# FoX attention: values multiplied as float16 halves, and the sums of the probabilities taken on TensorE in quarters of its columns

## The chip, the cores and the metric

One core of a Trainium2 chip runs the whole program in one launch. The metric is device time in microseconds (us), the median over runs. The engines are called by the profile's names: PE is TensorE (PEld its weight loads), DVE is VectorE, ACT is ScalarE, POOL is GpSimd, SP issues the DMAs. Each takes its own instructions in order and waits on semaphores for the others.

## What is computed

A decoder layer with three mixers side by side. The change concerns one of them, the forgetting attention (FoX): 8 heads of 64, 2048 queries (and 16 meta tokens ahead of them), swept in blocks.

```python
s = jnp.einsum('bhqd,bhkd->bhqk', qi, kf) * scale + cqi[..., None] - c[:, :, None, :]
mask = (kpos[None, :] <= qpos[:, None]) & valid[None, :]
p = jax.nn.softmax(jnp.where(mask, s, NEG), axis=-1)
return jnp.einsum('bhqk,bhkd->bhqd', p, vf)      # times silu(fg) afterwards
```

So every block needs the probabilities p, their product with the values v, and their row sums.

## The kernel before

The program runs in stages: norms and projections, the GLA mixer, the RG-LRU mixer, then FoX, then the output projection. `hybrid_kernel` writes a list of jobs; `merge` interleaves the main part of a job (for FoX, `fox_attend`) with the preparation of the next (`fox_prepare`) and, through the FoX stage, with a slow side job that prepares the output weights (`wout_ready`). A scheduler then sets each engine's order. The FoX stage has 16 jobs: 4 head pairs p, and for each 4 chunks c of 512 queries.

`fox_attend(p, c)` runs over blocks j of 128 keys, 4c+5 of them, so 5, 9, 13 and 17, and 176 in all. The last five of a chunk see fewer queries: 400, 272, 144 and 16 columns in place of 512. For each j:

- PE makes the logits of both heads in the PSUM pair `sq` (L1280, float16 high and low halves of keys and queries, and the forget terms `KX`), and adds the mask (L1286) on the diagonal. `sq` has one buffer, so the next j's logits wait for the exp of this one.
- ACT takes the exp of both heads into `pt`, float32, 1024 wide, a ring of three (L1288).
- DVE, and POOL for head 1 of every even j, add `pt` into the running sums `za` (L1293, L1296).
- PE multiplies values and probabilities, float32, into the PSUM bank `fv`: one matmul a head (L1304), each using 64 of the array's 128 columns. It does so for block j-2, behind the logits of block j; the last three come together at the end of the chunk.

After the last j, ACT copies the product (L1310), POOL multiplies it by the gate (L1311), PE sums `za` over its partitions (L1315, float32, the PSUM bank `fx`), and ACT copies that row (L506). Through a small DRAM buffer it is spread over the partitions, inverted on DVE (L1317, L1318), sent back and broadcast to `rz`, which POOL multiplies in (L1323).

`fox_prepare` for the next chunk makes the keys, queries and values (L485, L497), the values leaving PSUM by one ACT operation with a scale (L1173). It also finds each query's row maximum: PE makes logits in the pair `mq` (L1220, L1224, one buffer), DVE adds the forget terms and takes the maximum (L1228). The maxima are transposed through the bank `fx` (L1240) and sent by six small DMAs (L1251) into `QA`, where the attend's last logit matmuls read them.

## Time and profile before

| | us |
|---|---|
| median of 3 runs | 2014.05 (2011.25 to 2014.08) |
| the profiled execution | 2012.92 |
| its span | 2011.2 |
| the FoX stage in it, first logits to last sums | 915.2 to 1713.6, so 798.4 |

About 1.7 us lie outside the span. The profile's busy times and idle times are of this one execution. A matmul's end is modelled, so groups of matmuls of one kind show some 0.1 us more than the time to the next start; what a group takes from the engine is read from start to start. In the views below a pair of heads that runs at the same time shows as two matmuls, and a float32 matmul leaves two records, one for each of its two passes.

### The profile page before, as it was taken

The page shows a single profiled execution, that of the slowest core. Times are in us where ns is not written, and L with a number is a line of the kernel's source. Part 1 is how long each engine was busy: PE and PEld are TensorE (multiplying, and loading weights), DVE is VectorE, ACT ScalarE, POOL GpSimd, SP SyncE. Part 2 cuts the span into 40 slices and gives each one's busy share as a digit, 9 for nine tenths or more (in the row PEclk, how much of TensorE's full clock was granted, in tenths as well). Part 3 has the DMA queues.
Part 4 walks back from the last instruction along what each step waited for, and adds up shares of the span by engine and source line. Part 5 has one row for each costly group of instructions (what it writes and reads, how often), then busy time and mean ns, then how long its engine had stood idle before and what let it go on. Part 6 is the DMA issues. An engine that isn't in the chain of part 4 may idle for free.

```text
span 2011.2 us, 39461 instructions
## 1 busy us (share of the span) xinstructions
PE 1896.8 (94%) x15988; PEld 987.0 (49%) x15988; DVE 1271.7 (63%) x2834; ACT 1010.8 (50%) x1561; POOL 583.0 (29%) x564
## 2 busy tenths in 40 slices
PE   6889999999999999989999998899999988999998
PEld 5456666665555555545434442354335422444443
DVE  6756363444688778674565367756874665567664
ACT  7745553344888888762345233533442335444441
POOL 3434232332433333330122112221121124443432
PEclk9889999999999999999999999999999998999999
DMA  6200120211211110121132104321332108733411
GB/s 226 71 7 29 41 86 28 75 44 34 74 43 45 43 43 22 43 72 44 59 95 70 34 28 115 116 70 64 90 97 69 43 22 304 221 114 115 130 49 63
DMA packets 116134, 152.69 MB, mean 76 GB/s; under 512 B 18792, under 2 KB 75816, under 8 KB 115952
## 3 DMA queue, kind: packets, MB, share of 16 engines
q1 hardware_dynamic: 115952, 150.18, 23.4%
q8 instruction: 125, 2.05, 0.4%
q14 instruction: 57, 0.47, 0.1%
HBM read 108.71 MB, written 41.33 MB: 75 GB/s over the span
## 4 chain that ended last, share of the span: by engine, by line
PE 70%; DVE 9%; ACT 6%; issue 3%; POOL 3%; DMA 3%; SPq 0%; ACTq 0%; POOLq 0%; DVEq 0%
PE pj L485 28%; PE pj L1572 14%; PE pj L497 6%; PE fv L1304 6%; PE sq L1280 5%; PE mq L1220 2%; PE st L590 2%; DVE mj L1228 2%; ACT pt L1288 1%; PE gs L1028 1%; PE pv L1062 1%; DVE za L1296 1%; PE fx L1315 1%; DVE xc L563 1%; PE mq L1224 1%
## 5 line engine op out<-in xcount | busy, mean ns | idle before, releaser
L485 PE MATMUL pj<-xhl,whl 128*128 128x512 f16 (+3 forms) x3960 | 812.1, 356 | 10.8 <-ACT whl L437 6.3
L485 PEld LDWEIGHTS <-whl 128*128 128x128 f16 x3984 | 364.0, 98 | 396.0 <-issue 73.6
L1288 ACT ACTIVATE pt<-sq,consts 128x1024 f32<-128x1024 f32 (+4 forms) x176 | 163.3, 928 | 268.6 <-PE sq L1286 90.6
L1296 POOL TENSOR_TENSOR za<-za,pt 128x512 f32<-128x512 f32 (+1 forms) x80 | 101.0, 1262 | 548.1 <-ACT pt L1288 499.4
L1228 DVE CUSTOM_DVE_ANT_0 mj<-mq,CB 128x512 bf16<-128x512 f32 (+4 forms) x344 | 192.7, 580 | 63.0 <-PE mq L1220 31.1
L1572 PEld LDWEIGHTS <-whl 128*128 128x128 f16 x1344 | 130.6, 98 | 160.8 <-issue 4.5
L497 PEld LDWEIGHTS <-xhl 128*128 128x128 f16 (+1 forms) x3264 | 192.8, 100 | 33.6 <-issue 29.3
L497 PE MATMUL pj<-whl,xhl 128*128 128x128 f16 (+1 forms) x3024 | 197.6, 224 | 0.0
L1296 DVE TENSOR_TENSOR za<-za,pt 128x512 f32<-128x512 f32 (+3 forms) x208 | 121.5, 607 | 93.3 <-ACT pt L1288 90.2
L1304 PE MATMUL fv<-pt,fv 128*64 128x512 f32 (+4 forms) x688 | 175.1, 545 | 0.0
L1572 PE MATMUL pj<-xhl,whl 128*128 128x512 f16 x768 | 168.7, 380 | 0.0
L1280 PE MATMUL sq<-QA,KA 64*128 64x512 f16 (+4 forms) x1032 | 128.2, 344 | 12.3 <-ACT pt L1288 12.2
L1572 PE MATMUL pj<-ts,whl 128*128 128x512 f16 x576 | 125.7, 379 | 0.0
L563 DVE SCALAR_TENSOR_TENSOR xc<-lx,consts,xc 128x448 f32<-128x448 f32 (+1 forms) x120 | 93.7, 781 | 3.6
L1556 POOL TENSOR_TENSOR o<-o,xt 128x512 f32<-128x512 f32 x31 | 51.6, 1683 | 120.4 <-issue 91.7
L1538 ACT ACTIVATE sqo<-o 128x512 bf16<-128x512 f32 x32 | 20.1, 630 | 128.3 <-DVE o L1532 128.3
L1280 PEld LDWEIGHTS <-KA 64*128 64x128 f16 (+1 forms) x1032 | 40.3, 94 | 87.3 <-issue 65.5
L521 ACT ACTIVATE gate<-pj,consts 128x512 f32<-128x512 f32 (+2 forms) x72 | 46.1, 640 | 70.6 <-PE pj L485 58.5
L1578 DVE SCALAR_TENSOR_TENSOR o<-pj,consts,o 128x512 f32<-128x512 f32 x56 | 41.0, 744 | 60.5 <-PE pj L1572 56.3
L1220 PE MATMUL mq<-KA,QA 64*128 64x512 f16 (+4 forms) x344 | 60.8, 343 | 17.5 <-DVE consts L1228 15.1
L598 POOL TENSOR_TENSOR v<-a 128x448 f32<-128x448 f32 (+1 forms) x40 | 38.9, 973 | 129.4 <-ACT a L596 129.3
L522 DVE SCALAR_TENSOR_TENSOR gate<-gate,pj 128x512 f32<-128x512 f32 (+2 forms) x72 | 45.2, 627 | 40.8 <-ACT gate L521 40.7
(260 smaller groups left out, 2802.8 us busy)
## 6 DMA issues: line engine op xcount, KB each, us to landing
wr<-in_w_out_dram SPq DMA_DIRECT2D x64, 256.0 KB
y<-yD SPq DMA_DIRECT2D x32, 512.0 KB
raw<-in_w_grp_dram SPq DMA_DIRECT2D x28, 512.0 KB
wD<-ws SPq DMA_DIRECT2D x56, 256.0 KB
CB<-c32D SPq DMA_DIRECT2D x32, 256.0 KB
rawf<-in_w_grp_dram SPq DMA_DIRECT2D x16, 512.0 KB
xhl<-wD SPq DMA_DIRECT2D x16, 512.0 KB
xt<-in_x_dram SPq DMA_DIRECT2D x16, 512.0 KB
```

Of the source, the lines that this page charges most:

```text
L485: nc.tensor.matmul(out=ps, lhsT=a[:, kt, 0:m], rhs=b[:, kt, u0:u0 + n], start=i == 0, stop=i == 23)
L497: nc.tensor.matmul(out=ps, lhsT=a[:, kt, u0:u0 + m], rhs=b[:, kt, :], start=i == 0, stop=i == 23)
L521: k.act = nc.scalar.activation(out, ps, AF.Tanh, scale=hinv).ins
L563: nc.vector.scalar_tensor_tensor(out=xc, in0=lx[:, j:j + n], scalar=cw(j), in1=xc, op0=ALU.mult, op1=ALU.add)
L1220: nc.tensor.matmul(out=ps[h][:, 0:n], lhsT=qh[hs, P * i:P * i + P], rhs=d.hi[pc][hs, 0:n], start=True, stop=pc < c)
L1228: nc.vector.tensor_tensor_reduce(out=junk[:, h, 0:n], in0=ps[h][:, 0:n], in1=d.cb[pc][:, h, 0:n], scale=1.0, scalar=-3e38, op0=ALU.add, op ...
L1280: nc.tensor.matmul(out=sp[0:m, h, off:], lhsT=a[j // 4][hs, kk], rhs=b[hs, off:], start=i == 0, stop=i == 3 and d < 0)
L1288: k.exp = nc.scalar.activation(pt[0:m, :, off:], sp[0:m, :, off:], AF.Exp, scale=K.esc[0:m]).ins
L1296: eng.tensor_tensor(out=za[h][0:m, off:], in0=za[h][0:m, off:], in1=pt[0:m, h, off:], op=ALU.add)
L1304: nc.tensor.matmul(out=pv[hs, off1:], lhsT=V1[0:m1, j1 % 4, hs], rhs=pt1[0:m1, h, off1:], start=j1 == 0, stop=j1 == nj - 1)
L1556: eng.tensor_tensor(out=o, in0=o, in1=xt[:, h, :], op=ALU.add)
L1572: nc.tensor.matmul(out=ps, lhsT=a[:, kt, :], rhs=w[b + kt // 4][:, :, kt % 4, :], start=kt + j == 0, stop=(kt, j) == (KT - 1, 2))
```

## The change

The probabilities are lifted by 2^14 in the exp (a bias of 14 ln 2) and split on the spot: ACT copies them to float16 (`ph`, high half) and DVE subtracts to get the low half. The values are split in the same way when they leave PSUM, scaled by 2^-15. PE multiplies three of the four products of halves, and a float16 matrix of ones takes the sums: four matmuls a block (two halves by two heads), each using 32 of the array's columns and writing a quarter of a new PSUM bank `zb`. The adds on DVE and POOL, the buffers `za` and the sum matmuls at the chunk's end go; the bank `fx` becomes `zb`, and the transposed maxima go through `mq`. The end of a chunk sends four rows instead of two and adds two halves on DVE. The ring of `pt` shrinks to two, `ph` has three. In the output stage the loads of the last three weight blocks are ordered behind the send of these rows.

```diff
-PBUFS = {"pj": 2, "mx": 2, "st": 2, "pv": 2, "fx": 1, "fv": 1}
+PBUFS = {"pj": 2, "mx": 2, "st": 2, "pv": 2, "zb": 1, "fv": 1}
...
-    nc.scalar.activation(V[0:m, :, :], ps[0:m, 0:nb, :], AF.Copy, scale=wv[2][0:m])
+    split_pair(k, ps[0:m, 0:nb, :], V[0:m, 0], V[0:m, 1])
...
-    ps = bank(k, "fx")
+    ps = pair(k, "mq")[:, 0, :]
     nc.tensor.transpose(out=ps[0:8, 0:P], in_=mm, identity=k.ident)
...
-    za = [unit(k, "ZA", [P, CH], name="za") for _ in range(2)]
+    zb = bank(k, "zb")
...
-        pt = k.wk.tile([P, 2, CH], F32, name="pt", tag="PT", bufs=3)
+        pt = k.wk.tile([P, 2, CH], F32, name="pt", tag="PT", bufs=2)
+        ph = k.wk.tile([P, 2, 2, CH], F16, name="ph", tag="PH", bufs=3)
...
-        k.exp = nc.scalar.activation(pt[0:m, :, off:], sp[0:m, :, off:], AF.Exp, scale=K.esc[0:m]).ins
-        for h in range(2):
-            if j == 1:
...
-            elif j > 1:
-                eng = nc.gpsimd if h == 1 and j % 2 == 0 else nc.vector
-                eng.tensor_tensor(out=za[h][0:m, off:], in0=za[h][0:m, off:], in1=pt[0:m, h, off:], op=ALU.add)
...
+        nc.scalar.activation(pt[0:m, :, off:], sp[0:m, :, off:], AF.Exp, scale=K.esc[0:m], bias=k.lift[0:m])
+        k.exp = nc.scalar.copy(out=ph[0:m, 0, :, off:], in_=pt[0:m, :, off:]).ins
+        nc.vector.tensor_tensor(ph[0:m, 1, :, off:], pt[0:m, :, off:], ph[0:m, 0, :, off:], op=ALU.subtract)
+        todo.append((j, m, off, ph, V))
...
-                    nc.tensor.matmul(out=pv[hs, off1:], lhsT=V1[0:m1, j1 % 4, hs], rhs=pt1[0:m1, h, off1:],
-                                     start=j1 == 0, stop=j1 == nj - 1)
+                for i, (zv, zp) in enumerate(((0, 0), (1, 0), (0, 1))):
+                    for h in range(2):
+                        hs = slice(64 * h, 64 * h + 64)
+                        nc.tensor.matmul(out=pv[hs, off1:], lhsT=V1[0:m1, zv, j1 % 4, hs], rhs=ph1[0:m1, zp, h, off1:],
+                                         start=j1 == 0 and i == 0, stop=j1 == nj - 1 and i == 2)
+
+                for z in range(2):
+                    for h in range(2):
+                        r = slice(64 * z + 32 * h, 64 * z + 32 * h + 32)
+                        nc.tensor.matmul(out=zb[r, off1:], lhsT=k.onesh[0:m1], rhs=ph1[0:m1, z, h, off1:],
+                                         start=j1 == 0, stop=j1 == nj - 1)
...
-        nc.tensor.matmul(out=zp[hs, :], lhsT=k.ones[:, 0:64], rhs=za[h], start=True, stop=True)
-    D, zt = rows_spread(k, NCH * p + c, zp)
...
+    nc.scalar.copy(out=zs, in_=zb)
+    for z in range(2):
+        for h in range(2):
+            r = 64 * z + 32 * h
+            k.zdma = nc.sync.dma_start(out=D[z, h:h + 1, :], in_=zs[r:r + 1, :]).ins
...
+    nc.vector.tensor_tensor(zt[0], zt[0], zt[1], op=ALU.add)
...
-    k.mark = k.load
+    k.mark = k.zdma
```

The scheduler's new order is shown at three places. The first is PE in the middle of a late chunk, at a block with 400 columns. Before, in this place, the two float32 matmuls of the values (`fv`) follow the mask matmuls of a later block (L1286) and the next projection (L485) follows them:

```order
L1280 LDWEIGHTS KX
L1280 MATMUL sq<-QA,KX 128x144
L1286 LDWEIGHTS consts
L1286 MATMUL sq<-consts 128x128
L1304 MATMUL fv<-pt,fv 64x400 x2
L485 LDWEIGHTS whl
L485 MATMUL pj<-xhl,whl 128x512
```

Now the six float16 matmuls (of which the last two stand here) are followed by four of 32 columns into `zb`, and then by the next row-maximum logits (L1227, which was L1220):

```order
L1305 LDWEIGHTS fv
L1305 MATMUL fv<-ph,fv 64x400
L1311 LDWEIGHTS consts
L1311 MATMUL zb<-ph,consts 32x400
L1227 LDWEIGHTS QA
L1227 MATMUL mq<-KA,QA 128x512
```

Rows that repeat are left out: the pairs L1305 stand six times there and the pairs L1311 four times, each matmul with a weight load of its own. Where PE went from the values to other work at once, it now passes through a third form of matmul.

The second place is ACT in the last chunk of the stage, where the exps (`pt`) stand between the halves of the output stage's first operands (`whl`). Before:

```order
L1288 ACTIVATE pt<-sq,consts 128x1024
L1443 ACTIVATE whl<-y,consts 128x1024
L1288 ACTIVATE pt<-sq,consts 128x2x400
L1443 ACTIVATE whl<-y,consts 128x1024
L1443 ACTIVATE whl<-s_19338,consts 128x1024
L1288 ACTIVATE pt<-sq,consts 128x2x272
```

After, a cast to `ph` behind each exp (L1296 is the exp, L1460 the halves):

```order
L1296 ACTIVATE pt<-sq,consts 128x1024
L1297 CAST ph<-pt 128x1024
L1460 ACTIVATE whl<-y,consts 128x1024
L1296 ACTIVATE pt<-sq,consts 128x2x400
L1297 CAST ph<-pt 128x2x400
L1460 ACTIVATE whl<-y,consts 128x1024
```

The exp of 400 columns now has a cast and a half ahead of it instead of a half alone.

The third place is DVE in a late chunk, where the sums stand among the row maxima (`mj`) and the halves of the output weights (`ws`). Before:

```order
L1444 SCALAR_TENSOR_TENSOR ws<-wr,consts,ws 128x512
L1228 ISA mj,consts<-mq,CB 128x512
L1228 ISA consts 128x1
L1317 RECIPROCAL consts<-consts 128x8
L1318 TENSOR_SCALAR consts<-consts 128x8
L1293 TENSOR_TENSOR za<-pt 128x512 x2
```

After, one subtraction for both heads (L1298, here at a block of 144 columns) in the place of two adds, and the low half of the values (L1106) as a new operation; L1235 was L1228, L1461 was L1444:

```order
L1106 SCALAR_TENSOR_TENSOR fv<-pj,fv 128x512
L1298 TENSOR_TENSOR ph<-pt,ph 128x2x144
L1235 ISA mj,consts<-mq,CB 128x512
L1235 ISA consts 128x1
L1461 SCALAR_TENSOR_TENSOR ws<-wr,consts,ws 128x512
```

A row maximum that PE waits for can now stand behind a subtraction that itself waits for a cast.

## Rows read from the trace of the kernel before

**Rows 1.** Page of the profile, head and part 1: busy time, share of the span.

```profile
span 2011.2 us, 39461 instructions
PE 1896.8 (94%) x15988; PEld 987.0 (49%) x15988; DVE 1271.7 (63%) x2834; ACT 1010.8 (50%) x1561; POOL 583.0 (29%) x564
```

**Rows 2.** Stretches: length, then busy PE, PEld, DVE, ACT, POOL, granted clock, DMA.

```profile
1143.10:1189.60 46.50, 46.39 (x338) 19.91 (x338) 24.11 (x77) 15.04 (x26) 7.30 (x6) 1.00 0.04 13
1189.60:1245.10 55.50, 50.06 (x321) 17.29 (x322) 41.51 (x122) 23.41 (x32) 10.53 (x9) 0.94 0.30 92
...
1648.30:1713.60 65.30, 49.85 (x263) 14.56 (x262) 35.73 (x60) 31.02 (x37) 24.91 (x15) 0.85 0.74 250
915.20:1713.60 798.40, 755.09 (x5487) 314.08 (x5486) 498.70 (x1352) 311.78 (x454) 156.01 (x123) 0.98 0.27 84
```

**Rows 3.** Waits of PE in the FoX stage: us in total, times, longest.

```profile
PE mq L1220 <- DVE consts L1228: 13.9, 14, 3.7
PE sq L1280 <- ACT pt L1288: 12.2, 14, 3.0
```

**Rows 4.** Timeline of PE, one block: start, us, line, form, count.

```profile
1297.89 0.38 PE L1280 MATMUL sq<-QA,KX 64*128 64x512 bf16 x2
1298.20 1.08 PE L1304 MATMUL fv<-pt,fv 128*64 128x512 f32 x4
1299.21 0.96 PE L497 MATMUL pj<-whl,xhl 128*128 128x128 f16 x14
```

**Rows 5.** Timeline of PE, one head of a block by itself.

```profile
1290.87 1.07 PE L1304 MATMUL fv<-pt,fv 128*64 128x512 f32 x2
```

**Rows 6.** FoX stage, L1304, L1315 (PE, PEld), L1296 (DVE, POOL) alone, in turn.

```profile
915.20:1713.60 798.40, 176.01 (x704) 39.99 (x704) 0.98 0.27 84
...
915.20:1713.60 798.40, 19.24 (x64) 3.56 (x64) 0.98 0.27 84
...
915.20:1713.60 798.40, 121.48 (x208) 100.98 (x80) 0.98 0.27 84
```

**Rows 7.** Timeline of PE in earlier stages: matmuls of 48 and of 32 columns.

```profile
83.24 2.81 PE L633 MATMUL pj<-xhl,whl 128*48 128x256 f16 x48
85.98 0.82 PE L485 MATMUL pj<-xhl,whl 128*128 128x512 f16 x3
...
135.67 0.87 PE L1028 MATMUL gs<-lv 64*32 64x32 f32 x64 [0.33 <-DVE ac L1031]
```

**Rows 8.** Groups by line and form: count, busy us, mean ns, idle before.

```profile
L542 ACT CAST wrih<-wri 128x1024 fp32r<-128x1024 f32 x2 | 2.1, 1040 | 8.3 <-DMA wri<-in_w_i_dram 8.3
...
L1488 DVE TENSOR_TENSOR s<-s,y 128x1024 f32<-128x1024 f32 x8 | 9.7, 1216 | 6.8 <-POOL s L1487 6.7
...
L1100 DVE SCALAR_TENSOR_TENSOR KA<-pj,KA 128x512 f16<-128x512 f32 x16 | 11.0, 690 | 41.4 <-ACT KA L1099 41.4
```

**Rows 9.** Timeline of a late chunk: DVE alone, and beside POOL.

```profile
1308.15 0.74 DVE L1444 SCALAR_TENSOR_TENSOR ws<-wt,consts,ws 128x512 f16<-128x512 f32 x1
...
1310.26 1.78 POOL L1296 TENSOR_TENSOR za<-za,pt 128x512 f32<-128x512 f32 x1 [5.51 <-ACT pt L1288]
1310.83 1.76 DVE L1444 SCALAR_TENSOR_TENSOR ws<-wr,consts,ws 128x512 f16<-128x512 f32 x1
```

**Rows 10.** Timeline of the last chunk; in brackets the idle time before, and its cause.

```profile
1668.17 0.82 PE L1280 MATMUL sq<-QA,KA 64*128 64x512 f16 x6 [0.26 <-ACT pt L1288]
...
1669.30 1.11 ACT L1288 ACTIVATE pt<-sq,consts 128x1024 f32<-128x1024 f32 x1 [1.18 <-PE sq L1280]
...
1679.59 1.27 POOL L1323 TENSOR_TENSOR fo<-fo,rz 128x512 f32<-128x512 f32 x1 [4.72 <-DMA rz<-rowD]
...
1682.12 1.11 ACT L1288 ACTIVATE pt<-sq,consts 128x1024 f32<-128x1024 f32 x1 [3.15 <-POOL za L1296]
...
1683.28 0.82 PE L1280 MATMUL sq<-QA,KA 64*128 64x512 f16 x6 [2.21 <-ACT pt L1288]
```

**Rows 11.** Timeline of SP's queue as the output stage begins.

```profile
1723.65 0.91 SPq L1412 DMA_DIRECT2D ts<-wD  x2
```

More of the change, by code (lines that the diff above doesn't have):

```diff
@@ L261, in setup_constants @@
     nc.vector.memset(k.onesb, 1.0)
+    k.onesh = carve(k, 16).bitcast(F16)
+    nc.vector.memset(k.onesh, 1.0)
+    k.lift = carve(k, 1)
+    nc.vector.memset(k.lift, 14.0 * math.log(2.0))
     k.eps = carve(k, 1)
@@ L508, in rows_spread @@
         nc.sync.dma_start(out=D[0, h:h + 1, :], in_=zs[64 * h:64 * h + 1, :])
-    zt = small(k, "zt", [P, 8], bufs=2)
+    zt = small(k, "zt", [P, 8], bufs=4)
     nc.sync.dma_start(out=zt, in_=D[0].rearrange("h (q e) -> (h q) e", e=8))
@@ L1109, in fox_begin @@
     last = unit(k, "M", [P, 7 * NM + P], name="last")
-    d.lastV = last[:, 7 * NM:].rearrange("p (b v) -> p b v", b=1)
+    d.lastV = last[:, 7 * NM:].bitcast(F16).rearrange("p (z b v) -> p z b v", z=2, v=P)
     d.last = [last[:, NM // 2 * i:NM // 2 * (i + 1)].bitcast(F16) for i in range(2)]
```

27 lines of the change are left out of this document (13 added, 14 removed).

## The prediction, made before the changed kernel was run

> **What bounds the kernel now.** I read the shares of the page first: PE is busy 94% of the span, no other engine over 63% [rows 1]. The change touches the FoX stage alone, 798.4 us, so I cut that stage at the copies that end the chunks (L1310). Chunks of 5 and 9 blocks are PE's alone: the one from 1143.1 is 46.50 us long with PE busy 46.39, DVE 24.11 and ACT 15.04. Chunks of 13 blocks are less clear: 55.50 us with PE 50.06 and DVE 41.51. The last chunk, which has no next attention chunk to prepare, is bound by latency: 65.30 us to the end of the stage, PE 49.85, granted clock 0.85 [rows 2]. Over the stage PE is busy 755.09, DVE 498.70, ACT 311.78, POOL 156.01. Then the waits: PE waits most for DVE's row maxima (13.9 us) and for the exp (12.2 us) [rows 3]. So two questions decide: does the change take time from PE's own stream, and do the new operations on ACT and DVE make PE wait more.
>
> **PE's stream.** Logits, values and projection follow each other there without a wait [rows 4]: the float32 values of both heads take 1298.20 to 1299.21, 1.01 us, while the logit pair ahead, 512 columns of float16, takes 0.31 to the next start. Six such matmuls in three pairs take 0.66 up to it, 0.22 a pair, so 0.09 of the 0.31 is a change of the array's shape (64 rows to 64 columns). I find 0.09 to 0.10 at each change of that kind. The float32 pair itself is then 0.91, two passes of 0.43 and one weight load. One head by itself is as long as two together: 1.07 with its tail for one head, 1.08 for two [rows 4, 5]. So halves of the columns run at the same time when they stand next to each other, and a pair that the scheduler has torn apart costs a second 0.91.
>
> After, a full block has three float16 pairs at 0.216 and one quartet. That float16 halves run together is in the trace too: 48 matmuls of 48 columns by 256 take 83.24 to 85.98, 2.74 us [rows 7]. Less one change that is 0.110 a pair, the time of 256 columns once, with their weight loads hidden. For quarters there is only one poor row: 64 float32 passes of 32 columns by 32 in 0.87, which one quarter at a time, with both row halves at once, would need some 0.85 for without tail and change (32 times 0.027, from 0.43 for 512). I take the quartet as 0.216, since with the tail the row leaves about 0.7; the bounds are below.
>
> Sums, in blocks of 512: 112 blocks are full and 16 each have 400, 272, 144 and 16 columns; in pairs of float16 that is 30.1 us for all 176. Unbroken, before: the values 127 and the sums at the chunk ends (L1315) 16 times 0.91, 141 us. Unbroken, after: 30.1 times four, 120 us. To this come the torn groups, which I counted in the two orders: 18 us before, 12 after. So 159 becomes 132, **27 us less**. (The busy times, 176.01 and 19.24 [rows 6], are larger since they hold the tails.) Against it stand the changes of shape: a quartet is a third form beside halves of rows and halves of columns, and in the orders PE changes shape 845 times in the stage before and 1126 times after: 281 times 0.096 are **27 us more**. Logit pairs torn apart more often add 4. PE's own stream comes out at **+4 us**, where the work of the matmuls alone would promise a loss of 27.
>
> On the changes of shape the Trainium skill ("TensorEngine Tiling (Array Packing)", Key Properties) says that a change of the tiling mode, not of the tile alone, drains the engine; by that rule each quartet pays for coming and going. The row agrees, with 0.09 us for a change. Were only the changes between halves and quarters of columns free, 274 of them, the stream would come out at 22 us less; nothing in the rows suggests so.
>
> By chunks this +4 is uneven, and that matters, as PE's time counts fully only where PE binds. Counted in the same way, a chunk of 5 blocks gains 1 us of stream, one of 9 loses 2, one of 13 gains 3 to 5 (its quartets are torn most), one of 17 loses 3 to 4. Those of 13 have 5 us of room in the row above, so part of their gain is free.
>
> **ACT.** New: 176 casts. The nearest row is the cast of 1024 columns from SBUF, 1040 ns [rows 8]: 112 full ones are 116 us, the narrower ones some 34, together 150. ACT goes from 312 to 462 of 798 us, not the bound. Its cover is plainest in the last chunk, where ACT does nothing but exps for ten blocks: 1.11 us of exp, then 1.18 idle until the next logits [rows 10]. A cast of 1.04 fits, with 0.14 to spare; without that idle time it would cost 1.04 a block. The other copies there (squares and halves for the output stage) have no such room, and I put 2 us on the last chunk. The exp's bias operand has no row; it lies between nothing and 0.1 us an exp, and the idle 1.18 covers both ends but for the last 0.04.
>
> **DVE and POOL.** Out: 121.48 us of adds on DVE and 100.98 on POOL [rows 6]. In, on DVE: subtractions of 1024 columns at 1216 ns [rows 8], 112 times 1.22 is 137, the narrower ones 35; the low halves of the values, 16 at 690 ns and 4 small ones, 12; the adds and multiplies at chunk ends, about 7. DVE would go from 499 to 568. But POOL's adds slowed DVE: the same operation is 0.74 us alone and 1.76 beside an add on POOL [rows 9]. With all 80 adds gone that is between nothing and 80 times 1.02, 82 us; most of DVE's operations read PSUM and keep their time, and I take 25 off. So 543, 68%, spread as before. ACT also no longer waits for POOL: in the last chunk POOL stands 4.72 us for a DMA, the add behind it holds the `pt` buffer, the exp waits 3.15 and PE 2.21 [rows 10]. That wait goes; next late there is the chain of the sums' row on DVE, which stalls the same queue once a chunk while its DMA lands, as before. Of the 12.2 us that PE waits for exps in the stage [rows 3] I count two such places out of sixteen chunks' ends, **-4 us**.
>
> **What is added as waits.** The subtraction of block j waits for the cast, which waits for the exp; behind it in DVE's queue stand the row maxima, for which PE waits in `mq` [rows 3]. The exp of j+2 waits for the subtraction of j, with a ring of two where the adds had three. PE's value matmuls of j come two blocks later and need the low half. With 13.9 and 12.2 us of such waits now, and a chain longer by 1.04, I add a quarter to a third, **+7 us**; the bounds are nothing and the rival below. The rest lands on covers: three more small DMAs a chunk on SP stand ahead of the six that send the maxima, covered where PE still has projections; the moved weight loads are hardly moved, as SP issues the last of these loads at 1723.65 even now [rows 11], and they are wanted by the fifth product, four times 24 matmuls of 0.216 behind 1713.6, thus 1734. The transposed maxima take `mq` when its last reader is done anyway.
>
> Sum: 2012.9 + 4 + 2 - 4 + 7 is 2022; since part of the stream's gain in the 13-block chunks is free (2 us), **2020 us**. The profiled execution lies 1.1 us under the median of the runs, which I leave in the rounding.
>
> **Rivals.** *The stage gets faster.* If the relief counts in full: the 13.9 us of waits for the row maxima halved (-7) because DVE is not slowed by POOL, the two waits behind POOL gone (-5), the wait for the last sums gone and the stretches at half clock, 0.85 in the last chunk and 0.94 in the row above it [rows 2], shorter (-5), no new waits, and the stream's +4: 2000. For it speaks [rows 9]; against it, that DVE's total rises all the same.
>
> *The chain binds: slower.* Exp, cast, subtraction and values follow one another in every block, on queues that also carry other work. If each of the 120 blocks of the long chunks (13 and 17) loses the 0.26 us that PE loses in the last chunk's plain blocks [rows 10], that is 31 on top of the stream's +4, with the last chunk's +2 and the relief of 4 taken in: 2046. It decides once DVE's backlog ahead of a subtraction exceeds the time of about one block, 4 us; two row maxima, a half and a difference of output weights are 3 of that. For it: DVE busy 41.51 of 55.50 there [rows 2]. Against it: ACT's idle 1.18.
>
> *The quarters don't run together.* Two at a time, the quartets cost 38 us more: 2058; one at a time 113: 2133. The single row for them [rows 7] is narrow. The Trainium skill ("TensorE: Matmul & The Clock Gate", Measured speedup vs the span model) gives 2.38 times for three column tiles of 32 by 512; as an estimate from that, a quartet would take 0.27 or a little more in place of 0.216, and the whole 8 to 10 us more.
>
> **How the numbers follow.** I give the forecast 0.45 (2011 to 2031), the faster rival 0.27 (1992 to 2010), the chain 0.18 (2031 to 2050), the quarters 0.10. About 0.2%, 4 us, is what a measurement here can tell from no change. Of the forecast some 0.22 lies under 2018, within that; so faster 0.27, same 0.22, slower 0.51. The range leaves out the quarters and the lower third of the faster rival: 1999 to 2046.
>
> **What would show it.** In the changed profile: L1305's pairs 3 ns or so apart and 0.65 a full block; L1311's four together, 0.216, and 0.09 to 0.10 at each change; casts near 1.04 and subtractions near 1.22; the row maxima and halves on DVE never at 1.76 by POOL's adds; PE's waits for DVE and ACT in total near 33 us. It is wrong if the quartet takes 0.4 or more, if weight loads of the halves show between the matmuls, if L1305 waits for DVE's low half in most blocks, or if the 13-block chunks grow by more than 4 us each.

## The result: slower, and the profile after

The changed kernel took 2063.94 us (median of 4, 2053.64 to 2068.33) against 2014.07 for the kernel before: a ratio of 1.0245 (95% interval 1.0214 to 1.0277). The same kernel beside the later experiments (**e0_again**) took 2051.04, a ratio of 1.0199 (1.0183 to 1.0214). The prediction was 2020, with a range to 2046.

The page of the changed kernel's profile, answering [rows 1]: ACT has 160 us more, POOL 98 less, DVE and PE a little more.

```profile
span 2066.6 us, 41512 instructions
PE 1922.6 (93%) x16980; PEld 1023.3 (50%) x16980; DVE 1311.4 (63%) x2816; ACT 1170.9 (57%) x1737; POOL 485.5 (23%) x484
```

Stretches of the changed kernel, answering [rows 2], with the same columns: a 9-block chunk, a 13-block chunk, the last chunk with its sums, the stage:

```profile
1162.80:1207.50 44.70, 44.48 (x382) 20.85 (x381) 27.60 (x77) 22.87 (x35) 2.55 (x2) 1.00 0.04 14
1207.50:1268.20 60.70, 55.59 (x416) 21.26 (x416) 45.76 (x128) 36.88 (x47) 3.15 (x3) 0.97 0.28 89
1680.30:1758.30 78.00, 58.94 (x392) 20.98 (x389) 37.66 (x56) 48.25 (x56) 12.11 (x7) 0.87 0.44 152
926.70:1758.30 831.60, 775.95 (x6502) 349.08 (x6502) 533.33 (x1329) 473.86 (x632) 56.72 (x43) 0.98 0.25 75
```

The 9-block chunk is 2 us shorter, the 13-block one 5 longer, the last 13. From here a stage begins with its first logit matmul in `sq` and ends where ACT begins to copy the last product (before 917.9 to 1708.2, changed 926.7 to 1753.3), and what follows is the output stage. The 915.2 of the table of the kernel before is not a matmul but where the weight loads' queue waits, 2.7 us too early. The FoX stage goes from 790 to 827 and the output stage from 303 to 313; the other 9 us lie ahead of FoX, where nothing changed. In the repetition the stage began at 913.3, not at 926.7, so those 9 are chance. The stage of the repetition, its last chunk and its output stage:

```profile
913.30:1738.00 824.70, 770.49 (x6478) 347.33 (x6477) 532.62 (x1328) 472.59 (x630) 56.55 (x42) 0.98 0.24 75
1666.50:1738.00 71.50, 52.24 (x368) 19.05 (x368) 36.97 (x55) 47.18 (x54) 11.16 (x6) 0.88 0.45 155
1738.00:2049.20 311.20, 289.74 (x1344) 129.92 (x1342) 199.04 (x248) 116.76 (x195) 109.35 (x54) 0.97 0.39 125
```

What belongs to the change is 34 us in the FoX stage and some 8 behind it. PE's waits in the FoX stage of the changed kernel, answering [rows 3]:

```profile
PE fv L1305 <- DVE ph L1298: 25.1, 40, 4.0
...
PE sq L1288 <- ACT pt L1296: 4.7, 4, 3.2
PE fv L1305 <- ACT ph L1297: 4.0, 5, 1.5
PE mq L1227 <- DVE consts L1235: 3.0, 6, 1.3
```

The two waits of [rows 3], 26 us, have shrunk to 8; a new one, the values waiting for DVE's low half, is 25. Here is one such wait (PE's, ACT's and DVE's rows of one timeline of all engines, a 13-block chunk):

```profile
1229.50 1.05 ACT L1297 CAST ph<-pt 128x1024 f16<-128x1024 f32 x1
...
1231.17 0.62 PE L1305 MATMUL fv<-ph,fv 128*64 128x512 f16 x4
...
1231.72 0.39 PE L1311 MATMUL zb<-ph,consts 128*32 128x512 f16 x2
...
1232.83 0.69 DVE L1394 TENSOR_TENSOR wt<-wr 128x512 f32<-128x512 f32 x1 [2.62 <-DMA wr<-in_w_out_dram]
1233.44 1.22 DVE L1298 TENSOR_TENSOR ph<-pt,ph 128x1024 f16<-128x1024 f32 x1
...
1234.71 0.41 PE L1305 MATMUL fv<-ph,fv 128*64 128x512 f16 x2 [2.59 <-DVE ph L1298]
1235.05 0.39 PE L1311 MATMUL zb<-ph,consts 128*32 128x512 f16 x2
```

The cast ended at 1230.55. The subtraction could have begun then, but in DVE's queue a difference of raw output weights (L1394) stood ahead of it and waited 2.62 us for its DMA. So PE did two pairs of values, half of the sums, and stood. The Trainium skill ("TensorE: Matmul & The Clock Gate", Architectural detail: the array is 16× 32×32, not 1× 128×128) calls DVE's queue a strict FIFO; these rows agree. This is the second longest of the 40 waits; all but three are under 0.8 us.

The place also shows torn groups: four value matmuls and two of the sums, then the other two and two. An untorn block looks like this (PE's timeline):

```profile
1248.47 0.84 PE L1305 MATMUL fv<-ph,fv 128*64 128x512 f16 x6
1249.23 0.40 PE L1311 MATMUL zb<-ph,consts 128*32 128x512 f16 x4
1249.57 0.39 PE L491 MATMUL pj<-xhl,whl 128*128 128x512 f16 x1
```

It takes 0.76 for the values and 0.34 for the sums to the next start, 1.10 for a block (medians over the untorn blocks: 0.77 and 0.33). The quarters do run together: a pair by itself takes the same 0.33 (median of 30; 1235.05 is a pair), so a quartet torn in two pays twice.

In the last chunk's plain blocks nothing stands in DVE's queue, and the chain alone decides (timeline of PE, ACT and DVE, in order of time):

```profile
1714.66 0.41 PE L1305 MATMUL fv<-ph,fv 128*64 128x512 f16 x2 [0.64 <-DVE ph L1298]
...
1715.33 0.82 PE L1288 MATMUL sq<-QA,KA 64*128 64x512 f16 x6
...
1716.41 1.21 ACT L1296 ACTIVATE pt<-sq,consts 128x1024 f32<-128x1024 f32 x1 [0.61 <-PE sq L1288]
...
1717.65 1.04 ACT L1297 CAST ph<-pt 128x1024 f16<-128x1024 f32 x1
...
1717.78 0.82 PE L1288 MATMUL sq<-QA,KA 64*128 64x512 f16 x6
...
1718.73 1.23 DVE L1298 TENSOR_TENSOR ph<-pt,ph 128x1024 f16<-128x1024 f32 x1 [1.67 <-ACT ph L1297]
...
1718.75 0.62 PE L1305 MATMUL fv<-ph,fv 128*64 128x512 f16 x4
...
1720.01 0.41 PE L1305 MATMUL fv<-ph,fv 128*64 128x512 f16 x2 [0.64 <-DVE ph L1298]
```

Exp, cast and subtraction follow each other without a break, and PE's last pair starts 0.05 behind the subtraction. Two blocks take 5.35 us there (1714.66 to 1720.01), 2.68 a block, where the exp's 1.11 and its wait of 1.18 [rows 10] made 2.29 before.

These rows also show how far the values follow behind the logits. The exp at 1716.41 takes the logits of 1715.33, and its low half is what the pair at 1720.01 needs. Between them PE makes one block of logits (1717.78), not two. The program's text puts the values of block j-2 behind the logits of block j, but PE's order, which the scheduler sets, does not keep this everywhere. I counted it over the stage, without the last two blocks of each chunk, where no further logits come. In the chunks of 5 and 9 blocks the values stand two blocks behind. In those of 13 they stand one block behind at 41 of 44 places, in those of 17 at 24 of 60, 14 of them in the last chunk. All 40 waits for the low half are at these 65 places, and none is where the values stand two blocks behind. The kernel before had 33 of 44 and 26 of 60 such places already.

### The profile page after: what moved, and what is told of

Its sections match the earlier page's. It is cut to its first block, busy times and chain, and to the rows that moved or that the text cites. A ratio compares the mean times of both kernels' runs of the same rounds, so it can differ in the third digit from the quotient of the medians.

```text
span 2066.6 us, 41512 instructions
## 1 busy us (share of the span) xinstructions
PE 1922.6 (93%) x16980; PEld 1023.3 (50%) x16980; DVE 1311.4 (63%) x2816; ACT 1170.9 (57%) x1737; POOL 485.5 (23%) x484
## 4 chain that ended last, share of the span: by engine, by line
PE 64%; DVE 11%; ACT 7%; DMA 4%; issue 3%; POOL 3%; SPq 1%; ACTq 0%; DVEq 0%; POOLq 0%
PE pj L491 25%; PE pj L1589 13%; PE pj L503 6%; PE fv L1305 4%; PE sq L1288 4%; DVE ph L1298 3%; PE zb L1311 2%; PE mq L1227 2%; DVE mj L1235 2%; ACT pt L1296 1%; PE st L596 1%; ACT ph L1297 1%; PE gs L1034 1%; PE pv L1068 1%; POOL v L618 1%
## 5 line engine op out<-in xcount | busy, mean ns | idle before, releaser
L1296 ACT ACTIVATE pt<-sq,consts 128x1024 f32<-128x1024 f32 (+4 forms) x176 | 178.9, 1017 | 163.1 <-PE sq L1294 82.8
L1298 DVE TENSOR_TENSOR ph<-pt,ph 128x1024 f16<-128x1024 f32 (+4 forms) x176 | 180.9, 1028 | 125.0 <-ACT ph L1297 124.3
L1235 DVE CUSTOM_DVE_ANT_0 mj<-mq,CB 128x512 bf16<-128x512 f32 (+4 forms) x344 | 194.0, 582 | 86.9 <-PE mq L1227 49.6
L1305 PE MATMUL fv<-ph,fv 128*64 128x512 f16 (+4 forms) x1032 | 148.1, 354 | 30.1 <-DVE ph L1298 25.1
L1589 PE MATMUL pj<-xhl,whl 128*128 128x512 f16 x768 | 173.0, 385 | 3.0 <-ACT whl L1460 2.3
L1297 ACT CAST ph<-pt 128x1024 f16<-128x1024 f32 (+4 forms) x176 | 151.5, 861 | 6.6 <-POOL fo L1340 0.7
L1288 PE MATMUL sq<-QA,KA 64*128 64x512 f16 (+4 forms) x1032 | 133.5, 344 | 5.0 <-ACT pt L1296 4.7
L1318 POOL TENSOR_TENSOR fo<-fo,gate 128x512 f32<-128x512 f32 x16 | 21.2, 1325 | 363.6 <-ACT fo L1317 342.4
L1305 PEld LDWEIGHTS <-fv 128*64 128x64 f16 (+1 forms) x1032 | 51.0, 109 | 102.8 <-issue 83.0
L1573 POOL TENSOR_TENSOR o<-o,xt 128x512 f32<-128x512 f32 x31 | 52.7, 1719 | 118.2 <-issue 91.0
L1311 PE MATMUL zb<-ph,consts 128*32 128x512 f16 (+4 forms) x704 | 78.6, 346 | 0.1
L1340 POOL TENSOR_TENSOR fo<-fo,rz 128x512 f32<-128x512 f32 x16 | 23.4, 1461 | 230.8 <-DMA rz<-rowD 230.8
```

Of the source, the lines that this page charges most:

```text
L1235: nc.vector.tensor_tensor_reduce(out=junk[:, h, 0:n], in0=ps[h][:, 0:n], in1=d.cb[pc][:, h, 0:n], scale=1.0, scalar=-3e38, op0=ALU.add, op ...
L1288: nc.tensor.matmul(out=sp[0:m, h, off:], lhsT=a[j // 4][hs, kk], rhs=b[hs, off:], start=i == 0, stop=i == 3 and d < 0)
L1296: nc.scalar.activation(pt[0:m, :, off:], sp[0:m, :, off:], AF.Exp, scale=K.esc[0:m], bias=k.lift[0:m])
L1297: k.exp = nc.scalar.copy(out=ph[0:m, 0, :, off:], in_=pt[0:m, :, off:]).ins
L1298: nc.vector.tensor_tensor(ph[0:m, 1, :, off:], pt[0:m, :, off:], ph[0:m, 0, :, off:], op=ALU.subtract)
L1305: nc.tensor.matmul(out=pv[hs, off1:], lhsT=V1[0:m1, zv, j1 % 4, hs], rhs=ph1[0:m1, zp, h, off1:], start=j1 == 0 and i == 0, stop=j1 == nj ...
```

## The experiments

For each profile I added up PE's time in the FoX stage by kind of matmul, from each start to the next start, less the idle time that the trace shows. In us; "output" is from the copy of the last product to the end; the ratio is of the whole to the kernel before on the same chip. Each row but the median is from one profile; the first profile of the changed kernel has a stage of 826.6 and idle time of 55.6, so differences of 2 us say little.

| kernel | values | sums | maxima's logits | other matmuls | idle | stage | output | median, ratio |
|---|---|---|---|---|---|---|---|---|
| before | 166.6 | 16.0 | 57.1 | 509.9 | 41.0 | 790.6 | 303.0 | 2014.07 |
| changed (e0_again) | 131.9 | 64.9 | 62.1 | 511.3 | 54.3 | 824.5 | 311.2 | 2051.04, 1.0199 |
| e1_loads | 131.6 | 65.3 | 62.2 | 513.4 | 59.5 | 832.0 | 295.9 | 2045.96, 1.0167 |
| e2_later | 129.0 | 67.2 | 60.2 | 510.6 | 49.1 | 816.1 | 309.3 | 2040.60, 1.0148 |
| e3_nolow | 85.3 | 53.5 | 62.2 | 510.0 | 39.5 | 750.5 | 307.7 | 1975.74, 0.9826 |
| e4_nosums | 132.7 | 6.1 | 59.1 | 517.0 | 62.5 | 777.4 | 310.9 | 2006.63, 0.9980 |
| e5_two | 128.9 | 57.4 | 60.6 | 516.6 | 57.7 | 821.2 | 311.7 | 2048.16, 1.0181 |
| e8_halves | 106.9 | 87.6 | 60.6 | 513.3 | 57.6 | 826.0 | 306.1 | 2049.40, 1.0192 |
| e9_adds | 138.5 | 20.3 | 63.3 | 526.1 | 111.5 | 859.7 | 314.2 | 2091.49, 1.0404 |
| e10_free | 121.9 | 53.2 | 60.4 | 513.6 | 43.7 | 792.8 | 309.2 | 2019.57, 1.0033 |
| e11_nosub | 119.2 | 56.5 | 59.6 | 508.3 | 31.7 | 775.3 | 311.5 | 2004.37, 0.9961 |
| e7_beforelate | 164.9 | 15.1 | 57.2 | 507.7 | 36.8 | 781.7 | 310.3 | 2009.97, 0.9982 |
| e6_f16exp | 86.2 | 52.7 | 60.5 | 503.4 | 30.4 | 733.2 | 297.3 | 1948.88, 0.9680 |
| e12_f16wide | 68.4 | 50.5 | 61.2 | 504.1 | 33.4 | 717.6 | 297.3 | 1935.12, 0.9628 |
| e13_f16late | 68.9 | 50.5 | 61.2 | 506.3 | 33.7 | 720.6 | 307.8 | 1946.39, 0.9676 |

The change's 34 us are thus 35 less for the values, 49 more for the sums, 5 for the maxima's logits, 1 for the rest, and 13 of waits. Which cause makes them is what the runs are for.

### Is the first profile's delay part of the change? e0_again

> The changed kernel unaltered, for the same chip as the experiments. In its first profile the FoX stage began at 926.7, 9 us later than in the kernel before, although the work ahead is the same, while the four experiments run so far began it at 914.8 to 917.6. If the delay is chance (short half-clock stretches ahead of the stage fall otherwise in each execution), the stage begins within 914 to 920 here and the whole is 2045 to 2055, 36 to 48 above before. If it belongs to the change (the buffers' placement), it begins at 924 or later and the whole is 2060 or more.

Chance: the stage began at 913.3. All the other kernels of the table began it between 913.9 and 920.8.

### The chain: e2_later, e10_free, e11_nosub

**e2_later** moves the values one more block behind the logits in the program's text. (It also cuts the ring of raw output weights from six buffers to four.)

```diff
-        ph = k.wk.tile([P, 2, 2, CH], F16, name="ph", tag="PH", bufs=3)
+        ph = k.wk.tile([P, 2, 2, CH], F16, name="ph", tag="PH", bufs=4)
...
-        if len(todo) == 3 or j == nj - 1:
+        if len(todo) == 4 or j == nj - 1:
```

> Edit: the value matmuls of a block follow three blocks behind its logits instead of two, with four buffers of halves for three (a ring of raw output weights goes from six to four to make the room). Theory of the chain: PE's 25 us of waits for DVE's low halves in front of the values go to under 6, chunks of 13 blocks shrink from 58 on average to about 54, and the whole is 15 to 25 us below the changed kernel: 2040 to 2049. Rival (DVE as a whole, with its row maxima and subtractions, holds PE in these chunks): the waits move to the logits of the row maxima or to the exp, the chunks of 13 blocks stay within 1.5 us, and the whole is within 5 us of 2064. Rival (PE's own stream with the third array shape): the same as that, with no PE wait anywhere over 10 us.

In between. The waits for the low half fall from 25.8 to 15.6, but those for the maxima and the exp rise from 5.6 to 12.6; the stage gains 8 and the whole half a per cent. But the edit reached PE's order only in part: in the chunks of 13 blocks the values still stand one block behind the logits at 39 of 44 places, and in the last chunk at 14 of 15, and all 25 waits that are left are at places one block behind. So this run does not test what another block of time would do there. Waits of PE in the stage:

```profile
PE fv L1305 <- DVE ph L1298: 15.6, 25, 2.0
PE mq L1227 <- DVE consts L1235: 6.3, 13, 1.5
PE sq L1288 <- ACT pt L1296: 6.3, 10, 1.8
```

**e10_free** keeps all the work and takes PE's dependence on the low half away; **e11_nosub** takes the subtraction away as well.

```diff
# e10_free; e11_nosub has only the first line
-        nc.vector.tensor_tensor(ph[0:m, 1, :, off:], pt[0:m, :, off:], ph[0:m, 0, :, off:], op=ALU.subtract)
+        nc.vector.tensor_tensor(pl[0:m, :, off:], pt[0:m, :, off:], ph[0:m, 0, :, off:], op=ALU.subtract)
...
# in both:
-rhs=ph1[0:m1, zp, h, off1:]
+rhs=ph1[0:m1, 0, h, off1:]
...
-rhs=ph1[0:m1, z, h, off1:]
+rhs=ph1[0:m1, 0, h, off1:]
```

> Edit: the subtraction is still made, into a tile of its own, but nobody reads it: PE multiplies the high half again wherever it took the low one, so the result leaves out the low half of the probabilities while every engine's work stays. In the new order the groups of values and sums are torn less (200 and 180 for 246 and 226; 1016 changes of shape for 1126; 125.5 us of columns for 132.4), so values and sums fall by 18 us by the prices of the first profile. Chain theory (PE waits because the values need the low half): PE's waits for the subtraction go, the waits of the stage fall from 54 to about 40, and the stage from 825 to 790 to 795, the level of before. DVE theory (the subtraction is late because DVE has too much to do, and holds PE by the row maxima and the exp's buffers as well): the waits stay at 50 and only the 18 go: 805 or more.

> Edit: as the last, but the subtraction is not made at all (the low half of the probabilities is left out; PE's work stays, the high half read again). Against the last it takes only DVE's 165 us of subtractions away. Chain theory: no more than 5 us below the last, since DVE had room: 785 to 795. DVE theory: it goes 15 to 25 below the last, with PE's waits for the row maxima and exps together under 10.

The chain theory holds for the first step. Without the dependence the stage is 792.8, the level of before (790.6), with the same work on every engine. Of the 32 us, 11 are waits and 22 are values and sums, since their groups are no longer torn (200 and 180 groups in place of 246 and 226). Nothing else was edited, so the tears come from the dependence too: the order that I had taken as given holds the scheduler's answer to it. Waits of PE in **e10_free**:

```profile
PE mq L1227 <- DVE consts L1235: 9.1, 16, 2.4
PE fv L1306 <- ACT ph L1298: 7.9, 9, 1.9
PE sq L1289 <- ACT pt L1297: 7.8, 18, 1.9
```

The second step also counts: taking the subtractions off DVE (527 busy, then 367) is worth another 17.5, 12 of them waits. Here the DVE theory was right and my limit of 5 wrong, although its mark for the two waits was missed narrowly (11.5 in place of under 10). Waits of PE in **e11_nosub**:

```profile
PE sq L1288 <- ACT pt L1296: 6.8, 18, 1.0
PE mq L1227 <- DVE consts L1235: 4.7, 10, 1.3
```

### The parts alone: e3_nolow, e4_nosums, e9_adds

```diff
# e3_nolow
-        nc.vector.tensor_tensor(ph[0:m, 1, :, off:], pt[0:m, :, off:], ph[0:m, 0, :, off:], op=ALU.subtract)
...
-                for i, (zv, zp) in enumerate(((0, 0), (1, 0), (0, 1))):
+                for i, (zv, zp) in enumerate(((0, 0), (1, 0))):
...
-                for z in range(2):
+                for z in range(1):
```

> Edit: the low half of the probabilities is left out of the computation: no subtraction on DVE, two value products instead of three, sums of the high half alone (two of the four quarter matmuls, which take the time of four). PE's stream loses 138 blocks' worth of 0.216, 30 us. Stream theory: the whole falls by those 30 and nothing more: about 2034. Chain theory: the 25 us of PE's waits for the subtraction go as well, and DVE loses 170 us of work: 2064 - 30 - 25 = 2009 or a little less, with chunks of 13 blocks near 49.

The stage lost 74, more than the 55 of the chain theory: 47 in the values, of which the third product's columns are 30 and the untorn groups (185 in place of 246) the rest, 11 in the sums, 15 in waits, and no wait for a subtraction is left. The chain theory's sum left the torn groups out.

```diff
# e4_nosums
-                for z in range(2):
+                for z in range(2 if j1 == 0 else 0):
...
-    k.mark = k.zdma
+    k.mark = k.store
```

> Edit: the sums are left out of the computation but for the first block of each chunk (one quartet a chunk), and the late weight loads come behind the store of the last chunk, since the buffers do not fit otherwise; that can make the output stage longer, so the FoX stage is to be compared. PE's stream loses 160 quartets: 26 us for the columns, some 12 for quartets torn in two, and about 281 changes of the array's shape at 0.096, 27 us: 65 in all. Stream theory: the FoX stage falls from 835 to about 770. Chain theory: in chunks of 13 and in the last one PE only waits longer for the low half; with half of the gain of the 120 blocks of the long chunks lost the stage falls by 35 to 45, to about 795, and PE's waits in front of the values grow to 45 or more.

Between the two: the sums' 59 us go, 8 come back as waits and 6 in the other matmuls, and the stage is 777.4. The waits for the low half do not grow to 45 but stay at 26.3. So the sums on TensorE cost 47 net, and half-products without any sums would be 13 below the stage of before. Is it better, then, to leave the sums where they were?

```diff
# e9_adds
+                eng = nc.gpsimd if h == 1 and j % 2 == 0 else nc.vector
+                eng.tensor_tensor(out=za[h][0:m, off:], in0=za[h][0:m, off:], in1=pt[0:m, h, off:], op=ALU.add)
...
-                for z in range(2):
-                    for h in range(2):
-                        r = slice(64 * z + 32 * h, 64 * z + 32 * h + 32)
...
+        nc.tensor.matmul(out=zp[hs, :], lhsT=k.ones[:, 0:64], rhs=za[h], start=True, stop=True)
```

> One part alone: values multiplied as float16 halves, but the sums as in the kernel before (float32 adds on DVE and POOL, two matmuls at a chunk's end). To make room a ring of raw output weights goes from six to four, and the late weight loads stand behind the store of the last chunk, so the FoX stage is to be compared. PE: values and sums 197 become about 133 + 18. Stream theory: the stage is 827 - 46 = 781, under the 790 of the kernel before, so the change's loss is the sums on TensorE. DVE theory: the adds (121 us on DVE, 101 on POOL, which slows DVE) come on top of the subtractions; DVE is then busy some 690 of the stage, PE's waits for DVE grow from 30 to 60 or more and the stage stays at 805 to 825, so the subtraction is the loss and the sums on TensorE were needed to pay for it.

No: 4% above before, worse than either theory's figure. DVE is busy 678 of 860, and the waits for the low half double. (The cut ring of raw output weights is not the reason: **e2_later** has the same and a shorter stage than the changed kernel.) The stage's row, and the two largest waits in it:

```profile
915.30:1775.20 859.90, 748.24 (x5842) 333.22 (x5842) 678.12 (x1561) 473.18 (x632) 155.23 (x122) 0.97 0.23 72
```

```profile
PE fv L1315 <- DVE ph L1298: 51.2, 68, 4.7
PE mq L1227 <- DVE consts L1235: 24.1, 24, 3.0
```

The subtraction needs DVE's room, and the sums on TensorE are what makes that room. The two parts belong together, and together they lose.

### The price of a change of shape: e5_two, e8_halves, e12_f16wide

**e5_two** issues the quartets of two blocks behind every second block; **e8_halves** and **e12_f16wide** widen the ones, the latter in the version without a low half (below).

```diff
# e5_two
+                held.append((j1, m1, off1, ph1))
...
+                if j1 % 2 == 0 and j1 < nj - 1:
+                    continue
+                for j2, m2, off2, ph2 in held:
# e8_halves
-                        r = slice(64 * z + 32 * h, 64 * z + 32 * h + 32)
-                        nc.tensor.matmul(out=zb[r, off1:], lhsT=k.onesh[0:m1], rhs=ph1[0:m1, z, h, off1:],
-                                         start=j1 == 0, stop=j1 == nj - 1)
+                        r = slice(64 * h, 64 * h + 64)
+                        nc.tensor.matmul(out=zb[r, off1:], lhsT=k.onesh[0:m1], rhs=ph1[0:m1, z, h, off1:],
+                                         start=j1 == 0 and z == 0, stop=j1 == nj - 1 and z == 1)
# e12_f16wide, in e6_f16exp
-                        r = slice(64 * z + 32 * h, 64 * z + 32 * h + 32)
+                        r = slice(64 * h, 64 * h + 64)
```

> Edit: the sums' quartets are issued for two blocks together, behind every second block's values; the halves get four buffers for three. The order then has 172 groups of quarters in place of 226, 216 groups of values for 246, and 1047 changes of the array's shape for 1126. Stream theory (a group costs 0.118 beyond its columns, as in the profile of the changed kernel): the sums' matmuls fall from 64 to 57 us, the values' by 3, and the stage by 9 to 10. Chain theory: the same, and nothing more, since DVE's subtractions are as late as before; PE's waits for the low half stay at 20 to 28. Rival (a change of shape costs nothing by itself, the groups are slow for another reason, such as the weight loads): the sums stay at 63 or more.

> Edit: the sums use 64 columns of ones for each head in place of 32, both halves z into the same rows, so the third shape of the array is gone; the tail at a chunk's end sends two rows instead of four. Columns: by the order the groups of values and sums need 157.1 us of columns for 132.4, so 25 more; changes of shape 848 for 1126, so 278 fewer. At 0.118 each that is 33 less and the values and sums together fall from 197 to about 189; at the 0.096 of my prediction they come out even; if the change of shape from 64 columns to 32 costs nothing they rise by 25 to 221. The stage follows these to within 5 us, and the last chunk's tail is shorter by 1 to 2.

> The float16 version (e6) with the sums on 64 columns of ones a head in place of 32. PE's order is the same row for row and the columns that pass are the same (94.5 us for values and sums); only the third shape of the array goes: 1026 changes become 819. If a change costs 0.118, the FoX stage falls from 733 by 24 to 709 and the whole from 1949 to about 1925; at 0.096 by 20 to 713 and 1929. Rival (the quarters' groups cost their extra time for another reason than the change of shape, or PE would have waited there anyway): values and sums stay within 5 us of 139 and the whole within 6 us of 1949.

In **e5_two** values and sums fell by 10.5, as expected, but the stage by only 3: waits took 3 back and the other matmuls 5. In **e8_halves** they fell by 2.3 and the stage rose by 1.5; 25 us of columns against 278 changes come out like that at 0.097 a change. **e12_f16wide** measures it cleanly, with PE's order unchanged but for the width. One block of **e6_f16exp** and the same block of **e12_f16wide** on PE:

```profile
1247.19 0.62 PE L1302 MATMUL fv<-ph,fv 128*64 128x512 f16 x4
1247.74 0.39 PE L1308 MATMUL zb<-ph,consts 128*32 128x512 f16 x2
1248.07 0.82 PE L491 MATMUL pj<-xhl,whl 128*128 128x512 f16 x3
```

```profile
1238.14 0.62 PE L1302 MATMUL fv<-ph,fv 128*64 128x512 f16 x4
1238.60 0.38 PE L1308 MATMUL zb<-ph,consts 128*64 128x512 f16 x2
1238.91 0.82 PE L491 MATMUL pj<-xhl,whl 128*128 128x512 f16 x3
```

The four value matmuls take 0.55 to the sums of 32 columns and 0.46 to those of 64. Over the stage, values and sums fell by 20.0 us for 207 changes fewer: 0.097 each, and 15.6 of it reached the stage. The prediction's 0.096 holds for halves to quarters too; the 0.118 of my expectations also held something that is not the change of shape. The Trainium skill ("TensorEngine Tiling (Array Packing)", Key Properties) says that switching the tiling mode drains TensorE, without a figure; this is one for the change between halves and quarters.

### The late weight loads: e1_loads, e7_beforelate, e13_f16late

```diff
# e1_loads
-    k.mark = k.zdma
     for nm in BLOCKS[4:]:
+        k.mark = k.zdma if nm == BLOCKS[6] else k.load
# e7_beforelate, in the kernel before; e13_f16late, in e12_f16wide
-    k.mark = k.load
+    k.mark = k.zdma
```

> Edit: of the three late weight blocks the first two are again ordered as in the kernel before, behind the early loads; the third stays behind the send of the sums' rows (with all three early the buffers do not fit in SBUF). My theory of the output stage: it grew by 10 us (from the copy of the last product to the end 303 before, 313 after) because all twelve loads of those blocks were issued at 1754 to 1778 and the fifth product waited for them. Then the stage returns to 303 to 306, the FoX stage does not move, and the whole is 7 to 10 us below the changed kernel: about 2055. Rival: the output stage is longer because the clock fell to half in two stretches there that have another cause; then the wait for the weights goes but the stage stays at 311 to 315, and the whole within 4 us of 2064.

> The kernel before with one part of the change alone: the loads of the last three weight blocks ordered behind the send of the last sums' row. The change's output stage is 8 to 10 us longer (303 before, 311 to 313 after). If the late loads are the reason, the stage from the last copy of a product to the end is 309 to 313 here and the whole 2018 to 2022, 6 to 10 above before. If it is longer for another reason (the sums' longer tail, the halves of the output's operands that ACT now makes beside the casts), the whole stays within 3 of before.

> The same as the last, with the late weight loads behind the send of the sums' rows, as in the changed kernel. In the kernel before these loads made the last chunk 7 us shorter and the output stage 7 us longer, in sum nothing. Theory: the same here, the whole within 4 us of the last run. Rival: the early loads disturb the last chunk more where the chain is short, and the whole is 5 to 9 us lower; or the output stage waits for the weights, and it is 5 to 9 higher.

My theory fell as stated: in **e1_loads** the output stage is 296, below the 303 to 306 expected, and the FoX stage, which was not to move, is 7.5 longer. Put late, the loads make the output stage longer every time, by 7 in the kernel before, by 10 in the float16 version, by 15 between **e1_loads** and **e0_again**. Of these 15, 10 are idle time of PE (11.3, then 21.5), and 5 are the same 1344 matmuls taking longer (284.65, then 289.74), where the granted clock of the output stage is 0.97 in place of 0.99. So the rival with the clock was right in part; whether the waits bring the clock down or the clock has another cause is open. The waits themselves are mostly not for the weights. In **e0_again** PE waits there:

```profile
PE mx L478 <- DVE consts L476: 5.5, 1, 5.5
PE pj L1589 <- DMA ts<-wD: 3.5, 2, 3.4
```

The first is the scale of the next rows; the last loads of such rows stand behind the twelve weight loads in SP's queue, and I read the wait as coming from there, without a run that shows it. But what the output stage loses the last chunk may give back: it is 53.1 in place of 59.9 in **e7_beforelate** and 71.5 in place of 76.4 against **e1_loads**, and the whole is 0.2% lower in the first and 0.3% higher in the second. In **e13_f16late** the chunk stays at 52 and the whole is 11 higher, against the theory and more than the rival's 5 to 9. In **e7_beforelate** the last chunk also had a granted clock of 0.94 for 0.86 before, which may be part of its gain. What in the chunk pays for early loads I did not test. For the change it is a term of some 5 us (the intervals of the two ratios overlap), not of 10.

### A version that beats both: e6_f16exp

If the low half is the loss, the exp can write float16 directly.

```diff
-        nc.scalar.activation(pt[0:m, :, off:], sp[0:m, :, off:], AF.Exp, scale=K.esc[0:m], bias=k.lift[0:m])
-        k.exp = nc.scalar.copy(out=ph[0:m, 0, :, off:], in_=pt[0:m, :, off:]).ins
-        nc.vector.tensor_tensor(ph[0:m, 1, :, off:], pt[0:m, :, off:], ph[0:m, 0, :, off:], op=ALU.subtract)
+        k.exp = nc.scalar.activation(ph[0:m, 0, :, off:], sp[0:m, :, off:], AF.Exp, scale=K.esc[0:m], bias=k.lift[0:m]).ins
```

> A version that may beat both: the exp writes its float16 result directly, so there is no cast, no subtraction and no low half; the probabilities are rounded to float16 (this part of the precision is left out), the values keep both halves, the sums are those of the rounded probabilities (two matmuls of 32 columns a block), and the weight loads stand as in the kernel before, for which there is room now. By the order 190 groups of values with 62.7 us of columns and 185 of sums with 31.8: at 0.118 a group 139 us in place of 197. With the waits at 40 the stage is 825 - 58 - 14 = 753, the output stage 300, the whole about 1970, 2% below before. Rival: the last chunk stays bound by the exp and the sums' tail, so its waits stay at 19 and more and the whole ends at 1980.

It took 1948.88, 0.9680 of before (0.9665 to 0.9696), 21 us less than the theory said: values and sums are at the expected 139, but the waits are 30, not 40. With the wide ones (**e12_f16wide**) it is 1935.12, 0.9628 (0.9601 to 0.9655). These two give up the probabilities' low half. Of the versions that keep it and compute all the sums only **e7_beforelate**, the kernel before with its loads moved, lies below before, by 0.2%.

## Why the prediction was wrong, step by step

The step that failed is the term for the added waits, and with it the premise that PE's values of a block come two blocks after its logits. This holds in the program's text; in the order that PE runs they stand one block behind at 65 of the 104 places counted in the long chunks, and at 40 of these the chain of exp, cast and subtraction arrives too late. One of the prediction's own signs of being wrong came true: three of the four 13-block chunks grew by more than 4 us. The terms one by one:

- **PE's own stream, +4: measured +21** (values -35, sums +49, maxima's logits +5, the rest +1). The pieces held: halves and quarters run together, weight loads stay hidden, a change costs 0.097 for the 0.096 assumed, and torn logits cost 5 for 4. What was undersized is a group: six values take 0.77 for the 0.744 of the sum, a quartet 0.33 for 0.312, and with 472 groups in the trace these 0.02 are some 10 us. Another 5 are waits in disguise: in 26 places where the last pair waits inside its group, the group is 0.31 longer than its columns and not 0.12, since the time behind the modelled end of the pair ahead counts as busy. The kernel before was undersized in the same way, by some 6, so this closes only roughly.
- **The added waits, +7, less the relief, -4, and 2 for the last chunk: measured +13.** Both sides were far too small. The relief was 18: the waits for the maxima and the exp fell from 26 to 8 [rows 3]. The new waits were 29, for the low half (25) and the cast (4). This is the step that failed. I took a quarter to a third of the waits that were there, where the wait for the low half had no row, and gave the chain a chance of 0.18. Its condition was wrong too: I asked for a backlog of 4 us on DVE, and none was needed. In 23 of the 40 waits the subtraction starts within 0.15 us of its cast's end. There exp, cast and subtraction (1.20, 1.05 and 1.23, 3.5 us) are simply longer than PE's way over one block of logits to the pair that needs them: in the last chunk's rows PE was ready at 1719.37 (1718.75 and 0.62), 2.96 after the exp began. In the other 17 it starts 0.4 to 2.9 late, 14 times behind row maxima that had themselves waited for PE. That two blocks between would have been enough is supported by the 5- and 9-block chunks, which have no such wait, but no run shows it in the long ones.
- **Stream and waits as separate terms.** I read the torn groups from the order and priced them as PE's own. **e10_free** shows that they hang on the same lateness: 32 of the 34 us go when nobody waits for the low half. So the rival of the chain was right in its sign, but that its total (+31) fits is luck: it was 120 blocks at 0.26 of wait, and the runs show some 11 us of waits and 22 of tears.
- **The 13-block chunks, +3 to +5 each and partly free:** they grew by 7.3, 5.2, 8.0 and 3.1 in the first profile, together 23.6 of the stage's 36, and the room in them (5 us of PE idle in the one of [rows 2]) was not used.
- **ACT, nothing but 2: held as far as its load goes** (busy 474 for 462), though the cast is a third of the chain. A cast takes 1.045 (1.04 predicted); the exp with a bias 1.201 for 1.11, the upper end of the bound. **DVE at 543: measured 533**, with subtractions of 1.28 (1.22 predicted). That sum was right, but it says little about when a subtraction is done: most of the loss goes with the dependence (**e10_free**), and the load itself is worth another 17.5 (**e11_nosub**).

```profile
L1298 DVE TENSOR_TENSOR ph<-pt,ph 128x1024 f16<-128x1024 f32 x112 | 143.3, 1281 | 81.4 <-ACT ph L1297 80.8
L1296 ACT ACTIVATE pt<-sq,consts 128x1024 f32<-128x1024 f32 x112 | 134.5, 1201 | 94.7 <-PE sq L1288 65.9 <-PE sq L1294 16.1 <-DVE ph L1298 8.2
L1297 ACT CAST ph<-pt 128x1024 f16<-128x1024 f32 x112 | 117.1, 1045 | 4.6 <-POOL fo L1340 0.7 <-issue 0.4 <-PE zb L1311 0.2
```

- **The moved loads, "hardly moved": wrong by 5 to 10.** The row I relied on [rows 11] showed only the last of twelve. Eight had been issued by 1705 in the kernel before; here all twelve follow the sums' rows:

```profile
1754.36 0.24 SPq L1325 DMA_DIRECT2D rowD<-zs  x1
1754.69 1.78 SPq L1429 DMA_DIRECT2D ts<-wD  x3
...
1776.05 1.76 SPq L1429 DMA_DIRECT2D ts<-wD  x4
```

- **The quarters' rival** (2058 or 2133) did not come about, although its figure is near the result: a quartet takes 0.236 beside its change. The estimate that I made from the Trainium skill ("TensorE: Matmul & The Clock Gate", Measured speedup vs the span model), 0.27, was a little high.

## What to carry to other kernels

When a change puts two engines in series between a producer and PE, add up the bare chain and compare it with PE's way to the first matmul that needs the result; a wait comes even where every engine has room. Measure that way in the order PE runs, not in the program's text, since a scheduler can shorten the distance between a producer and its reader. Then look at what stands ahead of the new operation in its in-order queue, since an operation that waits for a DMA or for PE itself makes the chain as long as that wait. And do not price torn groups in the new order as a cost of their own: they can be the scheduler's answer to the same lateness, and go with it.

## What the hardware showed that I had not expected

- A change between halves and quarters of the array's columns costs PE 0.097 us, as one between rows and columns does, and it is paid in a pair as in a quartet: two matmuls of 32 columns take 0.326 to the next start, four take 0.332.
- A wait inside a group of matmuls seems to be some 0.19 us longer than the trace shows: a pair of the values is 0.41 long in its row while pairs that follow each other start 0.22 apart, and groups with a wait inside keep 0.19 more (0.96 for 0.77) after the shown wait is taken off.
- A float16 result costs the exp nothing: 1.203 for 1024 columns against 1.201 in float32, both with a bias operand, which costs 0.09.

```profile
L1295 ACT ACTIVATE ph<-sq,consts 128x1024 f16<-128x1024 f32 x112 | 134.7, 1203 | 136.9 <-PE sq L1287 111.0 <-PE sq L1293 24.5 <-issue 0.7
```
